# Gated DeltaNet block on one core: transpositions of k, q and v in one run for both heads of a pair, and longer steps between the interleaved pieces

## The chip, the cores and the metric

One Trainium2 chip; the kernel runs on one of its cores. The metric is the device time of one execution, in microseconds (us). The engines are called PE (matrix multiplication), DVE (vector), ACT (scalar), POOL (GpSimd) and SP (which issues most transfers).

## The reference

One layer, sequence 512, width 2048, float32. Two branches read one normalised input; the change touches the first.

```python
h = rmsnorm(x, g_pre)
proj = h @ w_in                       # q, k, v, z_a, beta, decay, conv input, gates
q, k, v = split(silu(causal_depthwise_conv(qkv, w_conv_qkv)))   # 4 taps, 16 heads x 128
q, k = l2norm(q), l2norm(k)           # x * rsqrt(sum(x*x) + EPS)
beta, g = sigmoid(b_raw), -exp(a_log) * softplus(a_raw + dt_bias)
# chunks of 64, per head: decay mask exp(gc_i - gc_j), triangular inverse T,
# then over 8 chunks: v_new = u - w S;  o = q_dec S + (q k^T * decay) v_new;
#                     S = S * exp(g_last) + k_end^T v_new
y_a = (rmsnorm(o_a) * silu(z_a)) @ w_br_a
u = causal_depthwise_conv(glu(...), w_dw) + b_dw                # 31 taps
y_b = (silu(layernorm(u)) * silu(z_b)) @ w_br_b
mixed = (gate_a * y_a + gate_b * y_b) @ w_out
x = x + rmsnorm(mixed)
x = x + rmsnorm(sigmoid(x @ w_ple_gate) * (p @ w_ple_proj))
```

## The kernel before, in words

**The large products.** Every float32 product is made of three passes in a reduced type: a weight tile is split into a rounded high part (L127, ACT) and the rest, the low part (L128, DVE; from the end of the heads on for a while POOL). `gemm_cm` makes one 128 x 512 output tile of the input projection, called g, from 16 blocks of weights with three matmuls each: L184 (high by high), L186 (high by low of the input hl), L188 (low of the weights by high). That is 48 matmuls to a tile. Two PSUM buffers (pool gps) take turns as g.

**What runs between them.** After each of these matmuls `tick()` is called. Side jobs are Python generators, entered by `spawn(gen, period)`. Each tick counts down each generator; when its count is out, the generator writes its next piece of instructions and yields again. A plain `yield` waits for the generator's period (4 ticks for a pair of heads, 5 for the decays), `yield n` for n ticks. So the code between two yields stands in one place of the program, and a longer wait puts the next piece behind more matmuls of g. `finish("heads")` drains what is left of the heads at the end of their stage, with no matmul between the pieces. The layer under the kernel may then reorder the instructions of an engine within limits; `pin` keeps some in place.

**The heads.** Sixteen heads are worked through in eight pairs, one pair per eight g tiles (384 ticks). For the pair g, `group(g)` makes, in this order: transposed k of both heads (pk, 4 transpositions of 128 x 128 each), from which ACT takes squares (junk, summed into sk) and DVE makes ke; the powers nk on POOL; transposed q (pq) and its squares into sq; transposed v (pv) and from it vh; the products pg of k and q; a product of sq with a constant that swaps halves of partitions (pe), from which comes epsq; the triangular inverse (prod, VT); the products py, pz, pd; and then two `head_scan` generators side by side, the recurrence over eight chunks (psA, psB, psS). A scan ends with squares of O, their power (ors, POOL), four products with the gate z (O, L739), a transposition back (po, L744) and its copy with a factor (oa, L749). While a scan of one pair runs out, `group` of the next pair has begun: their pieces meet.

**Buffers in PSUM.** Two buffers of the pool wps are shared in turn by all of pk, pq, pv, pg, pe, pz, py, pd, po and by the tiles of the decays (ba_t, gc_ps, sw_ps, r_ps). A new user waits until the last reader of the second-last one is done. The four buffers of sps serve the recurrence.

**The decays.** `beta_decay` runs once, ahead of the first pair. It makes the decays, a swapped copy of them (sw_ps, L614) and then, for the eight pairs, a mask each: products tg on DVE and POOL, a matmul pair into r_ps (L633), a chain on DVE and ACT on E_mk, and a store to DRAM (e_dram). E_mk has one buffer.

**Behind the heads.** The 31-tap filter of the second branch is done channel block by channel block: on DVE in steps of one tap (uc, L954), for two blocks on POOL (uc, L973, with the products pr from ACT). Finished blocks are added up on POOL; the first of them is a copy (acc, L918).

Of the kernel before, what the change touches and what calls it, by code (L numbers as in the profile page):

```python
# [9 lines left out]
F32 = mybir.dt.float32  # L10
F32R = mybir.dt.float32r
AF = mybir.ActivationFunctionType
ALU = mybir.AluOpType
AX = mybir.AxisListType.X

P = 128
T = 512
NTT = T // P
# [4 lines left out]
EPS = 1e-6  # L23
# [26 lines left out]
C_SWAP = 128  # L50
# [31 lines left out]
def _body(ctx, tc, A, out):  # L82
    nc = tc.nc
    PSUM = bass.MemoryType.PSUM
    mm = nc.tensor.matmul
# [12 lines left out]
    ident = cst[:, C_ID:C_ID + P]  # L98
# [7 lines left out]
    def cc(col, n=P):  # L106
        return cst[:, col:col + n]
# [406 lines left out]
    hd = heads_ctx.enter_context(tc.tile_pool(name="hd", bufs=2))  # L514
    wps = heads_ctx.enter_context(tc.tile_pool(name="wps", bufs=2, space=PSUM))
    sps = heads_ctx.enter_context(tc.tile_pool(name="sps", bufs=4, space=PSUM))
# [22 lines left out]
    def beta_decay(ps):  # L539
# [39 lines left out]
        s = tl("s")  # L579
# [29 lines left out]
        eg = tl("eg")  # L609
        nc.scalar.activation(eg, gcf, AF.Exp)  # L610
        nc.vector.tensor_scalar(neg_eg.rearrange("p t h -> p (t h)"), eg, -1.0, None, ALU.mult)
        yield
        pw = wps.tile([P, T], F32, tag="w", name="sw_ps")
        mm(pw[:, 0:n], cc(C_SWAP), eg, start=True, stop=True)  # L614
        nc.vector.tensor_copy(eg_sw.rearrange("p t h -> p (t h)"), pw[:, 0:n])
# [7 lines left out]
        for gi in range(NH // 2):  # L623
            tg = []
            for eng, src, tag in ((nc.vector, gh, "ke"), (nc.gpsimd, gl, "vh")):
                t = hd.tile([P, 2, NTT, 64], F32R, tag=tag, name="tg", bufs=2)
                gv = src.bitcast(F32)[:, :, 2 * gi:2 * gi + 2].rearrange("p t h -> p h t")
                eng.tensor_tensor(t, tri, gv.unsqueeze(3).broadcast_to([P, 2, NTT, 64]), ALU.mult)
                tg.append(t.rearrange("p h t i -> p (h t i)"))
            yield  # L630
            yield
            pr = wps.tile([P, T], F32, tag="w", name="r_ps")
            mm(pr, blk, tg[0], start=True, stop=False)  # L633
            mm(pr, blk, tg[1], start=False, stop=True)
            yield
            ed = hd.tile([P, 2, NTT, 64], F32, tag="W", name="E_mk", bufs=1)
            gcv = gc[:, :, 2 * gi:2 * gi + 2].rearrange("p t h -> p h t")
            nc.vector.tensor_tensor(ed, pr.rearrange("p (h t i) -> p h t i", h=2, i=64),
                                    gcv.unsqueeze(3).broadcast_to([P, 2, NTT, 64]), ALU.subtract)
            edf = ed.rearrange("p h t i -> p (h t i)")  # L640
            nc.vector.tensor_scalar(edf, edf, 0.0, None, ALU.min)
            nc.scalar.activation(edf, edf, AF.Exp)
            nc.vector.tensor_tensor(ed.rearrange("p h t i -> p (h t) i"), ed.rearrange("p h t i -> p (h t) i"),
                                    cst[:, C_TRI:C_TRI + 64].unsqueeze(1).broadcast_to([P, 8, 64]), ALU.mult)
            yield
            nc.sync.dma_start(e_dram[gi], edf)
# [38 lines left out]
    def head_scan(g, hh, G):  # L685
        h = 2 * g + hh
        st = hstate[h]
        kq, ke, vh = st["kq"], G["ke"][hh], G["vh"][hh]
        c_all = G["c"]
# [4 lines left out]
        for c in range(8):  # L694
            tt, par = divmod(c, 2)
            a, b = 64 * par, 64 - 64 * par
            x = hh * NTT + tt
# [30 lines left out]
        junk = hd.tile([P, P], F32, tag="junk", name="junk", bufs=1)  # L728
# [8 lines left out]
        yield  # L737
        for tt in range(NTT):
            nc.vector.scalar_tensor_tensor(O[:, tt, :], O[:, tt, :], rs2[:, tt:tt + 1], z[:, tt, :], ALU.mult, ALU.mult)  # L739
        yield  # L740
        yield
        po = wps.tile([P, NTT, 2, 64], F32, tag="w", name="po")
        for tt in range(NTT):
            nc.tensor.transpose(po[:, tt].rearrange("p x i -> p (x i)"), O[:, tt, :], ident)  # L744
# [7 lines left out]
    def group(g):  # L752
        G = dict(ke=[], vh=[])
# [3 lines left out]
        sq = hd.tile([P, 8], F32, tag="sq", name="sq")  # L757
        nk = hd.tile([P, 8], F32, tag="nk", name="nk")
        c_all = hd.tile([P, 8], F32, tag="c_all", name="c_all")
        W = hd.tile([P, 8, 2, 64], F32, tag="W", name="W", bufs=1)  # L760
        Ec = E.rearrange("p h t i -> p (h t) i")
        junk = hd.tile([P, P], F32, tag="junk", name="junk", bufs=1)
        heads = []
        for hh in range(2):
            h = 2 * g + hh
            heads.append((hh, h, slice(hh * NTT, (hh + 1) * NTT), hstate[h]["kq"], hstate[h]["kc"], hstate[h]["vc"]))
        for hh, h, s4, kq, kc, vc in heads:
            pk = wps.tile([P, NTT, P], F32, tag="w", name="pk")
            for tt in range(NTT):
                nc.tensor.transpose(pk[:, tt, :], kc[:, tt * P:(tt + 1) * P], ident)  # L770
            yield
            for tt in range(NTT):
                nc.scalar.activation(junk, pk[:, tt, :], AF.Square, accum_out=sk[:, hh * NTT + tt:hh * NTT + tt + 1])
            ke = hd.tile([P, NTT, P], F32, tag="ke", name="ke", bufs=2)
            nc.vector.tensor_tensor(ke, pk, ek[:, :, h:h + 1].broadcast_to([P, NTT, P]), ALU.mult)
            G["ke"].append(ke)
            nc.vector.tensor_scalar(sk[:, s4], sk[:, s4], EPS, None, ALU.add)
            nc.gpsimd.tensor_tensor(nk[:, s4], sk[:, s4], half_c[:, 0:NTT], ALU.pow)
            rk = hd.tile([P, NTT], F32, tag="rk", name="rk")
            nc.vector.reciprocal(rk, sk[:, s4])  # L780
            nc.vector.tensor_tensor(c_all[:, s4], rk, beta[:, :, h], ALU.mult)
            nc.gpsimd.tensor_tensor(Ec[:, s4, :], E[:, hh], c_all[:, s4].unsqueeze(2).broadcast_to([P, NTT, 64]), ALU.mult)
        for hh, h, s4, kq, kc, vc in heads:
            yield
            pq = wps.tile([P, NTT, P], F32, tag="w", name="pq")
            for tt in range(NTT):
                nc.tensor.transpose(pq[:, tt, :], kq[:, tt, 1:3, :].rearrange("p x i -> p (x i)"), ident)
            yield
            for tt in range(NTT):
                nc.scalar.activation(junk, pq[:, tt, :], AF.Square, accum_out=sq[:, hh * NTT + tt:hh * NTT + tt + 1])  # L790
        for hh, h, s4, kq, kc, vc in heads:
            pv = wps.tile([P, NTT, P], F32, tag="w", name="pv")
            for tt in range(NTT):
                nc.tensor.transpose(pv[:, tt, :], vc[:, tt * P:(tt + 1) * P], ident)
            yield
            vh = hd.tile([P, NTT, P], F32, tag="vh", name="vh", bufs=2)
            nc.vector.tensor_tensor(vh, pv, nk[:, s4].unsqueeze(2).broadcast_to([P, NTT, P]), ALU.mult)
            G["vh"].append(vh)
        yield
        pgs = []  # L800
        for hh, h, s4, kq, kc, vc in heads:
            pg = wps.tile([P, NTT, 2, 64], F32, tag="w", name="pg")
            for c in range(8):
                tt, par = divmod(c, 2)
# [5 lines left out]
        for hh, h, s4, kq, kc, vc in heads:  # L810
            nc.vector.scalar_tensor_tensor(W[:, s4, 0, :], pgs[hh][:, :, 0, :], -1.0, Ec[:, s4, :], ALU.mult, ALU.mult)
            nc.vector.tensor_tensor(W[:, s4, 1, :], pgs[hh][:, :, 1, :], Ec[:, s4, :], ALU.mult)
        pe = wps.tile([P, T], F32, tag="w", name="pe")
        mm(pe[:, 0:8], cc(C_SWAP), sq, start=True, stop=True)
        epsq = hd.tile([P, 8], F32, tag="epsq", name="epsq")
        nc.vector.tensor_scalar(epsq, pe[:, 0:8], EPS, EPS * P, ALU.add, ALU.mult)
        G.update(epsq=epsq, c=c_all)
        U = W[:, :, 0, :]
        QK = W[:, :, 1, :]

# [665 lines left out]
    ps = run(("P1",), stepper(gen))  # L1486
# [212 lines left out]
```

## Time and profile before

| | |
|---|---|
| median of 3 runs | 2446.0 us (2445.83 to 2446.65) |
| the profiled execution | 2447.55 us |
| its span in the trace | 2445.8 us, granted PE clock 0.998 |
| PE busy | 2414.0 us, 99% |
| PE's weight loads | 1985.5 us, 81% |
| DVE, ACT, POOL busy | 1792.4 (73%), 1208.8 (49%), 507.0 (21%) |

How to read the rows. In the timeline a row has the start in us from the span's beginning, the busy time, the engine, the line, the operation and "output<-inputs", and the shapes; "x4" means four in a row as one entry. A bracket gives the idle time of the engine just ahead of the row and what ended it. In the page's list of groups the numbers behind "|" are busy time in us and mean ns of one, and behind the next "|" the idle time ahead of the group and what ended most of it. In the list of waits stand the waiting instruction, what released it, and then total us, count and the longest. In a row of windows stand the stretch and its length, for each engine the busy time with the number of instructions in brackets (PE, weight loads, DVE, ACT, POOL), the granted PE clock, the DMA share and GB/s. A line such as "L775 ... x16: 681/688/693, 636.6 to 1391.9" gives the count, the shortest, middle and longest in ns, and the first and last start.

### The profile page before, as it was taken

To read this page: it belongs to the slowest core of one execution; us is meant where nothing else is said; L and a number is where in the kernel's file an instruction comes from. 1 tells how busy PE (TensorE), PEld (TensorE's weight loads), DVE (VectorE), ACT (ScalarE), POOL (GpSimd) and SP (SyncE) were. 2 spreads that over 40 slices of the span, in tenths; PEclk is the share of its full clock that TensorE was granted. 3 is DMA by queue.
4 is the path that set the end of the run, shared out by engine and by line. 5 is a ranking of instruction groups with operands and counts; after the bars stand their busy time and mean duration, and the time that the engine had idled before them with its cause. 6 is when DMAs were issued, how large, how long until landed. Compare 5 with 4: busy or idle time off the path is not lost.

```text
span 2445.8 us, 33732 instructions
## 1 busy us (share of the span) xinstructions
PE 2414.0 (99%) x11962; PEld 1985.5 (81%) x11962; DVE 1792.4 (73%) x3345; ACT 1208.8 (49%) x2357; POOL 507.0 (21%) x531
## 2 busy tenths in 40 slices
PE   8999999999999999999999998999999999999998
PEld 7888888887888888888888887888887888787886
DVE  7877888777677676867777678998998654667644
ACT  6455544554655656455555544454324533554532
POOL 0001110013213021132300005998740000000000
PEclk9999999999999999999999999999999999999999
DMA  7577776666536263556622222443534333665552
GB/s 270 162 199 199 202 201 208 207 162 204 175 119 185 87 185 93 171 168 178 181 90 90 67 91 79 138 137 104 170 118 166 131 122 99 232 216 173 188 173 77
DMA packets 145289, 380.21 MB, mean 155 GB/s; under 512 B 16352, under 2 KB 24800, under 8 KB 145120
## 3 DMA queue, kind: packets, MB, share of 16 engines
q1 hardware_dynamic: 119008, 319.32, 39.4%
q0 software_dynamic: 23808, 54.54, 10.3%
q10 hardware_dynamic: 2304, 4.20, 0.5%
q8 instruction: 94, 1.54, 0.3%
q14 instruction: 75, 0.61, 0.1%
HBM read 329.75 MB, written 48.23 MB: 155 GB/s over the span
## 4 chain that ended last, share of the span: by engine, by line
PE 89%; DVE 3%; POOL 2%; DMA 2%; issue 2%; ACT 2%; SPq 0%; POOLq 0%; DVEq 0%; ACTq 0%
PE g L186 13%; PE g L188 13%; PE g L184 13%; PE zp L423 6%; PE zp L421 6%; PE zp L422 5%; PE yp L1090 4%; PE yp L1094 4%; PE yp L1092 4%; PE f L1382 2%; PE f L1383 2%; PE f L1384 2%; PE f L1548 2%; PE f L1549 2%; PE f L1550 2%
## 5 line engine op out<-in xcount | busy, mean ns | idle before, releaser
L188 PE MATMUL g<-hh,w 128*128 128x512 f32 x1536 | 610.6, 397 | 4.1 <-POOL w L128 4.1
L186 PE MATMUL g<-hl,w 128*128 128x512 f32 x1536 | 611.3, 398 | 0.0
L184 PE MATMUL g<-hh,w 128*128 128x512 f32 x1536 | 609.5, 397 | 0.0
L127 ACT CAST w<-raw 128x512 fp32r<-128x512 f32 x588 | 357.9, 618 | 446.8 <-PE g L188 172.8
L128 DVE TENSOR_TENSOR w<-raw,w 128x512 fp32r<-128x512 f32 x464 | 321.5, 700 | 169.2 <-ACT w L127 166.6
L188 PEld LDWEIGHTS g<-hh,w 128*128 128x128 f32 x1536 | 289.8, 189 | 61.5 <-POOL w L128 5.4
L186 PEld LDWEIGHTS g<-hl,w 128*128 128x128 f32 x1536 | 289.6, 189 | 55.8 <-issue 1.4
L184 PEld LDWEIGHTS g<-hh,w 128*128 128x128 f32 x1536 | 289.9, 189 | 54.7 <-ACT w L127 0.9
L954 DVE SCALAR_TENSOR_TENSOR uc<-up,vec,uc 128x506 f32<-128x506 f32 (+29 forms) x390 | 284.0, 734 | 11.9
L128 POOL TENSOR_TENSOR w<-raw,w 128x512 fp32r<-128x512 f32 x124 | 161.4, 1314 | 136.7 <-DVE uc L954 74.5
L656 DVE SCALAR_TENSOR_TENSOR cv<-g,vec,cv 128x511 f32<-128x511 f32 x144 | 106.4, 739 | 27.2 <-ACT cv L654 26.6
L1090 PE MATMUL yp<-w,uh 128*128 128x512 f32 x256 | 100.2, 392 | 0.7 <-DVE gt L1102 0.7
L1094 PE MATMUL yp<-w,ul 128*128 128x512 f32 x256 | 100.1, 392 | 0.0
L1090 PE MATMUL yp<-w,oh 128*128 128x512 f32 x256 | 100.0, 393 | 0.0
L1092 PE MATMUL yp<-w,uh 128*128 128x512 f32 x256 | 100.0, 391 | 0.0
L1092 PE MATMUL yp<-w,oh 128*128 128x512 f32 x256 | 99.6, 389 | 0.0
L1094 PE MATMUL yp<-w,ol 128*128 128x512 f32 x256 | 99.1, 389 | 0.0
L842 DVE TENSOR_TENSOR prod<-UT,VT 128x2 f32<-128x2 f32 (+30 forms) x248 | 88.4, 356 | 6.5
L1006 POOL DMA_DIRECT2D wsum<-in_w_out x96 | 76.1, 847 | 71.2 <-DMA wsum<-in_w_out 32.9
L1326 POOL TENSOR_TENSOR rmsm<-totm,mhalf_c 128x2 f32<-128x2 f32 x2 | 2.4, 1198 | 378.3 <-DVE totm L1324 378.3
L973 POOL TENSOR_TENSOR uc<-uc,pr 128x511 f32<-128x511 f32 (+29 forms) x60 | 77.8, 1297 | 3.7 <-ACT pr L972 2.5
L1382 PE MATMUL f<-wsp,oph 128*128 128x512 f32 x192 | 75.6, 394 | 1.7 <-ACT wsp L1363 1.7
(386 smaller groups left out, 4952.5 us busy)
## 6 DMA issues: line engine op xcount, KB each, us to landing
raw<-in_w_in SPq DMA_DIRECT2D x194, 512.0 KB, 3.4
wsum<-in_w_out POOLq DMA_DIRECT2D x96, 256.0 KB, 5.4
raw<-in_w_ple_gate SPq DMA_DIRECT2D x40, 512.0 KB, 3.5
wo_sums<-wsum POOLq DMA_DIRECT2D x64, 256.0 KB, 4.1
raw<-in_w_br_a SPq DMA_DIRECT2D x32, 512.0 KB, 3.4
raw<-in_w_br_b SPq DMA_DIRECT2D x32, 512.0 KB, 3.3
raw<-in_w_ga SPq DMA_DIRECT2D x24, 512.0 KB, 4.7
raw<-in_w_gb SPq DMA_DIRECT2D x24, 512.0 KB, 4.5
```

The source lines that it names most:

```text
L127: nc.scalar.copy(hi, rq)
L128: low_part[0].tensor_tensor(lo, rq, hi.bitcast(F32), ALU.subtract)
L184: mm(ps, wh, rh, start=(k == 0), stop=False)
L186: mm(ps, wh, rl, start=False, stop=False)
L188: mm(ps, wl, rh, start=False, stop=(k == NK - 1))
L421: mm(ps[pr][t], lh, wh, start=q + n == 0, stop=False)
L423: mm(ps[pr][t], lh, wl, start=False, stop=q == 3 and n == 1)
L954: pin(nc.vector.scalar_tensor_tensor(y[:, s:], u[:, 0:T - s], vv(w0 + TAPS - 1 - s), y[:, s:], ALU.mult, ALU.add))
L1090: mm(ps[tt], lh[:, b], wh, start=k == 0, stop=False)
L1092: mm(ps[tt], lh[:, b], wl, start=False, stop=False)
L1094: mm(ps[tt], ll[:, b], wh, start=False, stop=k == NK - 1)
L1382: mm(ps, lh, wh[:, c], start=kk == 0, stop=False)
```

## The change

In `group`, a helper `turn(name, part)` writes the transpositions of k, q or v for both heads of the pair without a yield between them. The yields between the pieces become 6, 10, 6, 12 and 6 ticks in place of plain ones. The swap product pe and epsq move from behind pg into the piece of v, and pe's buffer comes from sps in place of wps. In `beta_decay` the swap of the decays comes 14 ticks after the piece before it, not 5, and each mask's r_ps 16 ticks after its products, not 10. In `head_scan`, po comes 16 ticks after the products O, not 8.

```diff
--- before.py
+++ after.py
@@ -609,7 +609,7 @@
         eg = tl("eg")
         nc.scalar.activation(eg, gcf, AF.Exp)
         nc.vector.tensor_scalar(neg_eg.rearrange("p t h -> p (t h)"), eg, -1.0, None, ALU.mult)
-        yield
+        yield 14
         pw = wps.tile([P, T], F32, tag="w", name="sw_ps")
         mm(pw[:, 0:n], cc(C_SWAP), eg, start=True, stop=True)
         nc.vector.tensor_copy(eg_sw.rearrange("p t h -> p (t h)"), pw[:, 0:n])
@@ -627,8 +627,7 @@
                 gv = src.bitcast(F32)[:, :, 2 * gi:2 * gi + 2].rearrange("p t h -> p h t")
                 eng.tensor_tensor(t, tri, gv.unsqueeze(3).broadcast_to([P, 2, NTT, 64]), ALU.mult)
                 tg.append(t.rearrange("p h t i -> p (h t i)"))
-            yield
-            yield
+            yield 16
             pr = wps.tile([P, T], F32, tag="w", name="r_ps")
             mm(pr, blk, tg[0], start=True, stop=False)
             mm(pr, blk, tg[1], start=False, stop=True)
@@ -737,8 +736,7 @@
         yield
         for tt in range(NTT):
             nc.vector.scalar_tensor_tensor(O[:, tt, :], O[:, tt, :], rs2[:, tt:tt + 1], z[:, tt, :], ALU.mult, ALU.mult)
-        yield
-        yield
+        yield 16
         po = wps.tile([P, NTT, 2, 64], F32, tag="w", name="po")
         for tt in range(NTT):
             nc.tensor.transpose(po[:, tt].rearrange("p x i -> p (x i)"), O[:, tt, :], ident)
@@ -764,11 +762,19 @@
         for hh in range(2):
             h = 2 * g + hh
             heads.append((hh, h, slice(hh * NTT, (hh + 1) * NTT), hstate[h]["kq"], hstate[h]["kc"], hstate[h]["vc"]))
+        def turn(name, part):
+            two = []
+            for hh, h, s4, kq, kc, vc in heads:
+                ps = wps.tile([P, NTT, P], F32, tag="w", name=name)
+                for tt in range(NTT):
+                    nc.tensor.transpose(ps[:, tt, :], part(tt, kq, kc, vc), ident)
+                two.append(ps)
+            return two
+
+        pks = turn("pk", lambda tt, kq, kc, vc: kc[:, tt * P:(tt + 1) * P])
+        yield 6
         for hh, h, s4, kq, kc, vc in heads:
-            pk = wps.tile([P, NTT, P], F32, tag="w", name="pk")
-            for tt in range(NTT):
-                nc.tensor.transpose(pk[:, tt, :], kc[:, tt * P:(tt + 1) * P], ident)
-            yield
+            pk = pks[hh]
             for tt in range(NTT):
                 nc.scalar.activation(junk, pk[:, tt, :], AF.Square, accum_out=sk[:, hh * NTT + tt:hh * NTT + tt + 1])
             ke = hd.tile([P, NTT, P], F32, tag="ke", name="ke", bufs=2)
@@ -780,19 +786,22 @@
             nc.vector.reciprocal(rk, sk[:, s4])
             nc.vector.tensor_tensor(c_all[:, s4], rk, beta[:, :, h], ALU.mult)
             nc.gpsimd.tensor_tensor(Ec[:, s4, :], E[:, hh], c_all[:, s4].unsqueeze(2).broadcast_to([P, NTT, 64]), ALU.mult)
+        yield 10
+        pqs = turn("pq", lambda tt, kq, kc, vc: kq[:, tt, 1:3, :].rearrange("p x i -> p (x i)"))
+        yield 6
         for hh, h, s4, kq, kc, vc in heads:
-            yield
-            pq = wps.tile([P, NTT, P], F32, tag="w", name="pq")
             for tt in range(NTT):
-                nc.tensor.transpose(pq[:, tt, :], kq[:, tt, 1:3, :].rearrange("p x i -> p (x i)"), ident)
-            yield
-            for tt in range(NTT):
-                nc.scalar.activation(junk, pq[:, tt, :], AF.Square, accum_out=sq[:, hh * NTT + tt:hh * NTT + tt + 1])
+                nc.scalar.activation(junk, pqs[hh][:, tt, :], AF.Square, accum_out=sq[:, hh * NTT + tt:hh * NTT + tt + 1])
+        yield 12
+        pvs = turn("pv", lambda tt, kq, kc, vc: vc[:, tt * P:(tt + 1) * P])
+        pe = sps.tile([P, P], F32, tag="s", name="pe")
+        mm(pe[:, 0:8], cc(C_SWAP), sq, start=True, stop=True)
+        yield 6
+        epsq = hd.tile([P, 8], F32, tag="epsq", name="epsq")
+        nc.vector.tensor_scalar(epsq, pe[:, 0:8], EPS, EPS * P, ALU.add, ALU.mult)
+        G.update(epsq=epsq, c=c_all)
         for hh, h, s4, kq, kc, vc in heads:
-            pv = wps.tile([P, NTT, P], F32, tag="w", name="pv")
-            for tt in range(NTT):
-                nc.tensor.transpose(pv[:, tt, :], vc[:, tt * P:(tt + 1) * P], ident)
-            yield
+            pv = pvs[hh]
             vh = hd.tile([P, NTT, P], F32, tag="vh", name="vh", bufs=2)
             nc.vector.tensor_tensor(vh, pv, nk[:, s4].unsqueeze(2).broadcast_to([P, NTT, P]), ALU.mult)
             G["vh"].append(vh)
@@ -810,11 +819,6 @@
         for hh, h, s4, kq, kc, vc in heads:
             nc.vector.scalar_tensor_tensor(W[:, s4, 0, :], pgs[hh][:, :, 0, :], -1.0, Ec[:, s4, :], ALU.mult, ALU.mult)
             nc.vector.tensor_tensor(W[:, s4, 1, :], pgs[hh][:, :, 1, :], Ec[:, s4, :], ALU.mult)
-        pe = wps.tile([P, T], F32, tag="w", name="pe")
-        mm(pe[:, 0:8], cc(C_SWAP), sq, start=True, stop=True)
-        epsq = hd.tile([P, 8], F32, tag="epsq", name="epsq")
-        nc.vector.tensor_scalar(epsq, pe[:, 0:8], EPS, EPS * P, ALU.add, ALU.mult)
-        G.update(epsq=epsq, c=c_all)
         U = W[:, :, 0, :]
         QK = W[:, :, 1, :]
```

In the built programs an ordinary pair has 39 runs of small matmuls before and 36 after, and r_ps follows r_ps every 26 ticks, not 20. Three places in the order of the engines, with the buffer numbers in the names:

PE, the meeting of the first and the second pair (po is the end of the first, all others belong to the second; matmuls of g stand in the places left out). Before:

```order
L744 MATMUL po_6730<-cst_75,O_6325 128x128 x4
L744 MATMUL po_6735<-cst_75,O_6331 128x128 x4
...
L770 MATMUL pk_6779<-cst_75,kc_6065 128x128 x4
...
L770 MATMUL pk_6800<-cst_75,kc_6445 128x128 x4
...
L787 MATMUL pq_6826<-cst_75,kq_6067 128x128 x4
...
L787 MATMUL pq_6843<-cst_75,kq_6447 128x128 x4
...
L794 MATMUL pv_6865<-cst_75,vc_6278 128x128 x4
...
L794 MATMUL pv_6876<-cst_75,vc_6755 128x128 x4
...
L807 MATMUL pg_6891<-kq_6067 64x128 x8
L807 MATMUL pg_6900<-kq_6447 64x128 x8
...
L814 MATMUL pe_6920<-sq_6774,cst_75 128x8
```

After (L770 is the line of all transpositions in the helper):

```order
L770 MATMUL pk_6763<-cst_75,kc_6063 128x128 x4
L770 MATMUL pk_6768<-cst_75,kc_6425 128x128 x4
...
L742 MATMUL po_6805<-cst_75,O_6334 128x128 x4
...
L742 MATMUL po_6810<-cst_75,O_6340 128x128 x4
...
L770 MATMUL pq_6830<-cst_75,kq_6065 128x128 x4
...
L770 MATMUL pq_6835<-cst_75,kq_6427 128x128 x4
...
L770 MATMUL pv_6875<-cst_75,vc_6273 128x128 x4
L770 MATMUL pv_6880<-cst_75,vc_6739 128x128 x4
L798 MATMUL pe_6885<-sq_6758,cst_75 128x8
...
L816 MATMUL pg_6904<-kq_6065 64x128 x8
L816 MATMUL pg_6913<-kq_6427 64x128 x8
```

Both pk now stand ahead of both po, and each pq behind the po of the same number; pe stands with pv.

DVE at the same place (cv are the steps of a 4-tap filter on a finished g, w a low part, O and oa the end of the first pair). Before:

```order
L739 SCALAR_TENSOR_TENSOR O_6325<-O_6325,ors2_6699,za_6326 128x128 x4
...
L739 SCALAR_TENSOR_TENSOR O_6331<-O_6331,ors2_6703,za_6332 128x128 x4
...
L749 TENSOR_SCALAR oa_6744<-po_6730,vec_76 128x4x64 x2
L749 TENSOR_SCALAR oa_6747<-po_6735,vec_76 128x4x64 x2
L656 SCALAR_TENSOR_TENSOR cv_6750<-g_6602,vec_76,cv_6750 128x511
L128 TENSOR_TENSOR w_6763<-raw_6758,w_6763 128x512
L656 SCALAR_TENSOR_TENSOR cv_6750<-g_6602,vec_76,cv_6750 128x510
L775 TENSOR_TENSOR ke_6792<-pk_6779,ek_4983 128x512
L656 SCALAR_TENSOR_TENSOR cv_6750<-g_6602,vec_76,cv_6750 128x509
...
L775 TENSOR_TENSOR ke_6813<-pk_6800,ek_4983 128x512
...
L797 TENSOR_TENSOR vh_6874<-pv_6865,nk_6775 128x512
L797 TENSOR_TENSOR vh_6885<-pv_6876,nk_6775 128x512
```

After:

```order
L655 SCALAR_TENSOR_TENSOR cv_6734<-g_6588,vec_76,cv_6734 128x511
L128 TENSOR_TENSOR w_6747<-raw_6742,w_6747 128x512
L655 SCALAR_TENSOR_TENSOR cv_6734<-g_6588,vec_76,cv_6734 128x510
L781 TENSOR_TENSOR ke_6783<-pk_6763,ek_4983 128x512
L655 SCALAR_TENSOR_TENSOR cv_6734<-g_6588,vec_76,cv_6734 128x509
...
L747 TENSOR_SCALAR oa_6820<-po_6805,vec_76 128x4x64
...
L781 TENSOR_TENSOR ke_6795<-pk_6768,ek_4983 128x512
...
L747 TENSOR_SCALAR oa_6820<-po_6805,vec_76 128x4x64
...
L747 TENSOR_SCALAR oa_6823<-po_6810,vec_76 128x4x64 x2
...
L806 TENSOR_TENSOR vh_6896<-pv_6875,nk_6759 128x512
L801 TENSOR_SCALAR epsq_6894<-pe_6885 128x8
L806 TENSOR_TENSOR vh_6898<-pv_6880,nk_6759 128x512
```

The copies oa have moved from ahead of the filter and both ke to places between and behind the ke; epsq comes between the two vh.

POOL behind the heads, around the first copy into acc (uc and pr are the filter's block on POOL, w a low part). Before:

```order
L973 TENSOR_TENSOR uc_14138<-uc_14138,pr_14211 128x509
L973 TENSOR_TENSOR uc_14138<-uc_14138,pr_14241 128x508
L128 TENSOR_TENSOR w_14249<-raw_14247,w_14249 128x512
L128 TENSOR_TENSOR w_14252<-raw_14247,w_14252 128x512
L973 TENSOR_TENSOR uc_14138<-uc_14138,pr_14277 128x507
L128 TENSOR_TENSOR w_14294<-raw_14292,w_14294 128x512
L918 COPY acc_14450<-uc_13756 128x512
L128 TENSOR_TENSOR w_14297<-raw_14292,w_14297 128x512
L973 TENSOR_TENSOR uc_14138<-uc_14138,pr_14313 128x506
L128 TENSOR_TENSOR w_14336<-raw_14334,w_14336 128x512
```

After:

```order
L128 TENSOR_TENSOR w_14248<-raw_14246,w_14248 128x512
L128 TENSOR_TENSOR w_14251<-raw_14246,w_14251 128x512
L977 TENSOR_TENSOR uc_14137<-uc_14137,pr_14276 128x507
L128 TENSOR_TENSOR w_14293<-raw_14291,w_14293 128x512
L128 TENSOR_TENSOR w_14296<-raw_14291,w_14296 128x512
L977 TENSOR_TENSOR uc_14137<-uc_14137,pr_14312 128x506
L922 COPY acc_14456<-uc_13764 128x512
L128 TENSOR_TENSOR w_14335<-raw_14333,w_14335 128x512
L128 TENSOR_TENSOR w_14338<-raw_14333,w_14338 128x512
L977 TENSOR_TENSOR uc_14137<-uc_14137,pr_14346 128x505
```

One low part and one step of the filter that followed the copy now stand ahead of it.

## The prediction

> **What bounds the kernel now.** I read the page first, then who waited for whom on PE, then the timeline at the places that the change touches.
>
> ```profile
> span 2445.8 us, 33732 instructions
> PE 2414.0 (99%) x11962; PEld 1985.5 (81%) x11962; DVE 1792.4 (73%) x3345; ACT 1208.8 (49%) x2357; POOL 507.0 (21%) x531
> ...
> L188 PE MATMUL g<-hh,w 128*128 128x512 f32 x1536 | 610.6, 397 | 4.1 <-POOL w L128 4.1
> ```
>
> PE is the bound from end to end. Work on the other engines costs nothing until PE waits for it, so every term below is a wait or a restart of PE. These are PE's waits at the places in question:
>
> ```profile
> PE g L188 <- POOL w L128: 4.1, 2, 3.5
> PE po L744 <- DVE O L739: 3.1, 4, 1.0
> ...
> PE r_ps L633 <- DVE E_mk L638: 0.7, 1, 0.7
> ...
> PE sw_ps L614 <- ACT ba_s L610: 0.6, 1, 0.6
> PE pv L794 <- ACT junk L790: 0.2, 1, 0.2
> ```
>
> The changed places own little: some 4.6 us in total. The four po waits are all in the last pair of heads. The largest wait, 3.5 us at L188, lies behind the heads, but its queue is one that the change reorders.
>
> **The runs of transpositions.** PE, an ordinary pair (the second):
>
> ```profile
> 738.82 1.04 PE L744 MATMUL po<-cst,O 128*128 128x128 f32 x8
> 739.61 0.48 PE L188 MATMUL g<-hh,w 128*128 128x512 f32 x1
> 739.92 0.40 PE L184 MATMUL g<-hh,w 128*128 128x512 f32 x1
> ...
> 741.52 0.60 PE L770 MATMUL pk<-cst,kc 128*128 128x128 f32 x4
> 741.88 0.48 PE L186 MATMUL g<-hl,w 128*128 128x512 f32 x1
> 742.20 0.40 PE L188 MATMUL g<-hh,w 128*128 128x512 f32 x1
> 742.43 0.40 PE L184 MATMUL g<-hh,w 128*128 128x512 f32 x1
> ```
>
> The first column is the start. A run of eight takes 0.79 us to the next g matmul and 0.31 to the one after; plain ones follow each other in 0.23. A run of four takes 0.36 and 0.32. Eight transpositions with two matmuls behind them are 0.79 + 0.31 + 0.23 = 1.33 us as one run, 2 x (0.36 + 0.32) = 1.36 as two. So a run saved is worth 0.03 us at most. The built programs have 39 runs of small matmuls per pair before and 36 now: 3 x 8 x 0.03 = 0.7 as the upper end, nothing as the lower. I take -0.4, as the four hundredths are near the rounding. The swap product pe costs the same two passes wherever it stands; its new home sps takes it out of the wps rotation.
>
> The Trainium skill ("TensorE: Matmul & The Clock Gate", section Single matmul latency) gives a lone matmul a fixed 166 ns beyond its columns, which a stream hides. If each run paid that, 24 fewer runs would be worth, as an estimate from that page, 4.0 us, and the sum would be 3.6 us lower. The rows above disagree: a run costs hundredths.
>
> **The masks.** The chain of one mask ends in a store, and the next mask waits for its buffer:
>
> ```profile
> 582.62 0.68 DVE L638 TENSOR_TENSOR E_mk<-r_ps,gc 128x512 f32<-128x512 f32 x1
> ...
> 632.14 0.69 DVE L638 TENSOR_TENSOR E_mk<-r_ps,gc 128x512 f32<-128x512 f32 x1 [0.98 <-DMA e_dram<-E_mk]
> ...
> 610.37 0.39 PE L184 MATMUL g<-hh,w 128*128 128x512 f32 x1
> 611.51 0.47 PE L633 MATMUL r_ps<-tg,blk 128*128 128x512 f32 x1 [0.75 <-DVE E_mk L638]
> ```
>
> Seven steps take 49.5 us, 7.07 each. PE offered a step every 20 matmuls, 20 x 0.23 + 0.5 = 5.1 us, ran out of wps buffers once and lost 1.14 - 0.23 = 0.9 us. At 26 matmuls it offers one every 6.5 us. With two buffers' head start (14 us) the lag of 7 x 0.57 = 4 us never reaches PE. Gain 0.9; bounds 0.9 and 0. The chain now ends about 1.4 us later, since its first step starts 13 matmuls (3.0 us) later and no longer sits behind DVE; the second pk is ordered behind it. The longer wait at the swap of decays moves nothing: sw_ps stands behind the same ACT instructions and after the same g matmul in both orders, so its 0.6 us stays. The first pair's pv wait (0.2 us) gives way to waits of the same kind; I take 0 with 0.6 either way.
>
> **The meeting of two pairs.** In seven of eight pairs the po of the finished pair now stands behind the k of the next, and all these share the two wps buffers: po[0] needs pk[0] read out, po[1] pk[1], pq[0] po[0], pq[1] po[1]. Before, eight matmuls stood between po and pk and nobody waited. What a pk needs to come free:
>
> ```profile
> 742.22 0.28 ACT L773 ACTIVATE junk<-pk 128x128 f32<-128x128 f32 x1 [0.22 <-PE pk L770]
> ...
> 745.57 0.20 ACT L773 ACTIVATION_READ_ACCUMULATOR junk<-pk 128x1 f32 x1
> ...
> 743.83 0.69 DVE L775 TENSOR_TENSOR ke<-pk,ek 128x512 f32<-128x512 f32 x1 [0.28 <-ACT junk L773]
> 744.43 0.74 DVE L656 SCALAR_TENSOR_TENSOR cv<-g,vec,cv 128x509 f32<-128x509 f32 x1
> ...
> 740.50 0.87 DVE L749 TENSOR_SCALAR oa<-po,vec 128x256 f32<-128x256 f32 x2
> ...
> 641.38 0.66 PE L794 MATMUL pv<-cst,vc 128*128 128x128 f32 x4 [0.23 <-ACT junk L790]
> ...
> 745.18 0.60 PE L787 MATMUL pq<-cst,kq 128*128 128x128 f32 x4
> ...
> L775 DVE TENSOR_TENSOR ke<-pk,ek x16: 681/688/693, 636.6 to 1391.9; 128x512 f32<-128x512 f32 x16
> ```
>
> Times from pk's start at 741.52: squares from 0.70, ke only after four of them, 2.31 to 3.00. ACT and DVE hold the same instructions ahead of these now, so pk[0] is free at 3.00. PE comes to po[0] after eight g matmuls: 0.79 + 0.31 + 7 x 0.23 = 2.71. It waits 0.29, and a run after a wait takes 0.06 longer (0.66 against 0.60): 0.35 us. Then po[1], seven matmuls on, at 3.05 + 0.36 + 0.32 + 6 x 0.23 = 5.11. The eighth square ends at 4.25, the second ke would at 5.04: even. pq[0] follows at 5.79; oa of the first head, whose second half stands behind that ke, ends by 5.75: even. pq[1] at 7.39, oa of the second at about 7.42. Three even ones, 0.1 together. 0.45 x 7 = +3.1 us. The lower end is 0 (the buffer is handed over before ke ends). The upper takes one more DVE instruction of 0.60 in front of one of the even ones: 0.95 x 7 = 6.7. Behind that, pv comes 13 matmuls (3.4 us) after pq[1] and needs only the four squares of that head; eight with a cast between them took 742.22 to 745.77. pg comes ten after pv, 2.6 us: covered.
>
> **The last pair.** Its end is issued in one go when the stage closes; five g matmuls more now cover it, and half a step of the recurrence more lies in it.
>
> ```profile
> 738.05 1.14 DVE L739 SCALAR_TENSOR_TENSOR O<-O,ors,za 128x128 f32<-128x128 f32 x4 [1.12 <-POOL ors L735]
> ...
> 1486.03 2.16 DVE L739 SCALAR_TENSOR_TENSOR O<-O,ors,za 128x128 f32<-128x128 f32 x4 [1.19 <-POOL ors L735]
> ...
> 1486.48 1.29 POOL L128 TENSOR_TENSOR w<-raw,w 128x512 fp32r<-128x512 f32 x1 [0.49 <-ACT w L127]
> ```
>
> Four O products take 1.14 us in an ordinary pair and 2.16 beside POOL's L128. POOL now has both powers of the last pair next to each other, so the first four lose this companion: -1.0. The tighter recurrence may wait 0.3 more. I take -0.7; bounds -1.5 and +1.5.
>
> **The low part behind the heads.** POOL makes the low parts of weights (L128) there and also adds up filtered channels. Its copy acc waits for a whole channel on DVE, with the next low part behind it:
>
> ```profile
> 1495.02 3.50 POOL L973 TENSOR_TENSOR uc<-uc,pr 128x511 f32<-128x511 f32 x2 [2.47 <-ACT pr L972]
> ...
> 1510.25 1.72 POOL L128 TENSOR_TENSOR w<-raw,w 128x512 fp32r<-128x512 f32 x1
> 1519.40 0.61 POOL L918 COPY acc<-uc 128x512 f32<-128x512 f32 x1 [7.43 <-DVE uc L954]
> 1519.97 1.27 POOL L128 TENSOR_TENSOR w<-raw,w 128x512 fp32r<-128x512 f32 x1
> ...
> 1494.17 6.58 DVE L954 SCALAR_TENSOR_TENSOR uc<-sg,vec,uc 128x502 f32<-128x502 f32 x5
> ...
> 1507.51 11.83 DVE L954 SCALAR_TENSOR_TENSOR uc<-sg,vec,uc 128x493 f32<-128x493 f32 x12
> ...
> 1517.45 0.39 PE L186 MATMUL g<-hl,w 128*128 128x512 f32 x1
> 1521.29 0.79 PE L188 MATMUL g<-hh,w 128*128 128x512 f32 x1 [3.45 <-POOL w L128]
> ...
> 1526.96 0.40 PE L184 MATMUL g<-hh,w 128*128 128x512 f32 x1
> ...
> 1521.30:1526.00 4.70, 4.70 (x11) 3.73 (x12) 4.49 (x7) 0.04 (x1) 4.70 (x4) 0.50 0.65 217
> ```
>
> From 1495.02 POOL does ten pieces of 1.70 us, then stands until 1519.40. A DVE channel step takes 0.75 us alone and 1.69 beside POOL: two alone and three beside make the 6.58 of the first row, nine and three the 11.83 of the second. Now POOL has a low part and a step more ahead of the copy (12 x 1.70 = 20.4 us), all starts 5 x 0.23 = 1.15 later, and DVE has 22 steps and an evacuation left, not 21. Before, DVE did 1.1 steps alone and 10.1 beside POOL until POOL stood at 1512.0; the other 9.8 end at 1519.4 by this reckoning, and 1519.34 is what happened. Now it does 1.1 and 12.1 until 1516.6; the other 8.8 take 6.6, the evacuation 0.6, which is 1523.8. Copy and low part take 1.9 as before (1519.34 to 1521.24): 1525.7. PE needs this low part 12 matmuls later than the old one: 1517.68 + 2.73 = 1520.4. Wait 5.3 against 3.6: +1.7. The granted clock is 0.50 in the row after the wait (PEclk, third from the end): the 13 intervals from 1521.29 to 1526.96 take 5.67 us, 2.7 above 13 x 0.23. I keep that. Bounds: wait and slow clock gone, -6.3; two more DVE steps beside POOL, +3.
>
> **Sum.** -0.4 - 0.9 + 0 + 3.1 - 0.7 + 1.7 = +2.8 us. The profiled execution took 2447.55 (its span and 1.75 around it), so 2450.35 there; that execution stands 1.55 above the median of 2446.0, so I predict 2448.8. A measurement of this kernel can tell about 0.2%, 4.9 us, from no change.
>
> **Rivals.** (a) The meeting costs nothing because the hand-over is earlier than I read it: without 3.1 the time is 2445.7. The pq of before, which started at 745.18 without a wait, 0.66 after ke was done, can't exclude it. (b) Slower: at the meeting the order on DVE lets one 0.60 us instruction in front of the second ke, and po[1], pq[0] and pq[1] wait in turn: 6.7 in place of 3.1, 2452.4. From 0.74 us per meeting on it is slower by more than 0.2%. Against it: ke took 681 to 693 ns in all sixteen heads (the last row above), so DVE was met in the same state each time. (c) Faster: the channel on DVE is done before PE asks for the low part, as POOL's extra pieces run while DVE waits for something else; wait and slow clock vanish: 2448.8 - 1.7 - 6.3 = 2440.8. It needs the channel 5.3 us earlier than worked out. (d) The long wait breaks in two: the evacuation that stands between the last channel steps holds a g bank, so PE stops twice, and the clock may stay up: 2448.8 - 2.7 = 2446.1.
>
> For (d) the Trainium skill ("TensorE: Matmul & The Clock Gate", section Why this matters for your kernels) says that idle gaps beyond about 3 us bring half rate. By that rule the trace agrees so far: 3.45 us of idle time was followed by 0.50.
>
> **Chances.** Forecast 0.46, with its own range 2446.5 to 2451.5; (a) 0.18; (b) 0.16; (c) 0.08; (d) 0.12. Slower by over 0.2%: (b) and 0.06 of the forecast's upper tail, 0.22. Faster: (c), 0.08. Within: 0.70. The range reaches from between (c) and (a), 2443.5, to just past (b), 2453.
>
> **What would show it.** PE waits at the first po of seven pairs for ke, 0.3 us each; no r_ps wait; sw_ps still 0.6; acc on POOL near 1523.8 plus what PE has lost until then; a clock row near 0.5 behind it. Wrong if po finds its buffer free, or if the low part's wait is much off 5.3.

## The result and the profile after

The changed kernel takes 2467.5 us (median of 4 runs, 2466.6 to 2470.2) against 2446.0: ratio 1.009, 95% interval 1.0078 to 1.0102. It is 21.5 us slower; the forecast was +2.8 and a range up to 2453.

The waits of PE in the profile after (what waited, on what, total us, times, longest):

```profile
PE py L867 <- DVE Tc L861: 3.9, 9, 1.0
PE g L188 <- POOL w L128: 3.2, 1, 3.2
PE po L742 <- DVE O L738: 3.2, 2, 1.7
PE pz L870 <- DVE Tc L861: 2.0, 7, 0.3
PE po L742 <- DVE ke L781: 2.0, 7, 0.3
PE psB L708 <- DVE Xz L704: 1.9, 6, 0.3
...
PE sw_ps L614 <- ACT ba_s L610: 0.7, 1, 0.7
```

What was forecast is there: seven waits of po for ke, 0.3 us each, sw_ps much as before (0.6 us before, 0.7 now), no r_ps. What was not is py, pz and psB: the inverse and the recurrence, which the change doesn't touch.

Listed waits are only part of such a loss, since a run that is broken by a wait also costs its restart: in the rows below, py and pz lose 1.45 us with 0.68 us of listed waits. So I added up, for the stretch of 3820 g matmuls from the decays on, all time between the starts of PE instructions beyond 0.227 us per g matmul, and booked it to the small matmuls at which it lies ("g": between two g matmuls only). This table is worked out from all PE rows of each profile, in us:

```
kernel      masks  k,q,v,po,pg  py,pz,pd  recurrence     g     sum
before       7.5      52.3        25.2       86.8      10.9   182.7
after        6.7      55.1        36.2       91.6      13.7   203.1
```

Of +20.4, the inverse's products have +11.0, the recurrence +4.8, the meetings of pairs +2.7, g itself +2.8, the masks -0.8. (The spans of the two profiles differ by 19.0; the remaining 1.4 us came back outside this stretch.) Per ordinary pair: py, pz, pd 3.11 to 4.6, recurrence 10.82 to 11.6, k to pg and po 5.92 to 6.4.

The inverse in the second pair, first PE, then DVE, and before also ACT. Before:

```profile
797.91 0.39 PE L186 MATMUL g<-hl,w 128*128 128x512 f32 x1
798.23 0.69 PE L863 MATMUL py<-Tc,W 32*32 32x32 f32 x32
798.85 1.15 PE L866 MATMUL pz<-W,Tc 64*64 64x64 f32 x32
799.93 0.50 PE L188 MATMUL g<-hh,w 128*128 128x512 f32 x1
...
793.48 0.67 DVE L850 STREAM_TRANSPOSE Vd<-VT 128x256 f32<-128x256 f32 x1
794.08 0.71 DVE L656 SCALAR_TENSOR_TENSOR cv<-g,vec,cv 128x511 f32<-128x511 f32 x1
...
797.04 1.37 DVE L857 STREAM_TRANSPOSE Tc<-VP 32x256 f32<-32x256 f32 x3
...
794.19 2.83 ACT L856 COPY VP<-Vd 32x256 f32<-32x256 f32 x4 [3.26 <-DVE Vd L850]
```

After:

```profile
800.43 0.39 PE L184 MATMUL g<-hh,w 128*128 128x512 f32 x1
800.88 0.21 PE L867 MATMUL py<-Tc,W 32*32 32x32 f32 x2
801.49 0.69 PE L867 MATMUL py<-Tc,W 32*32 32x32 f32 x30 [0.39 <-DVE Tc L861]
802.25 0.30 PE L870 MATMUL pz<-W,Tc 64*64 64x64 f32 x2
802.83 1.14 PE L870 MATMUL pz<-W,Tc 64*64 64x64 f32 x30 [0.29 <-DVE Tc L861]
803.90 0.51 PE L186 MATMUL g<-hl,w 128*128 128x512 f32 x1
...
794.82 0.74 DVE L655 SCALAR_TENSOR_TENSOR cv<-g,vec,cv 128x511 f32<-128x511 f32 x1
...
797.30 0.75 DVE L655 SCALAR_TENSOR_TENSOR cv<-g,vec,cv 128x509 f32<-128x509 f32 x1
797.96 0.42 DVE L847 TENSOR_REDUCE VT<-prod 128x8 f32<-128x256 f32 x1
...
798.88 0.67 DVE L854 STREAM_TRANSPOSE Vd<-VT 128x256 f32<-128x256 f32 x1
800.30 0.43 DVE L861 STREAM_TRANSPOSE Tc<-VP 32x256 f32<-32x256 f32 x1 [0.75 <-ACT VP L860]
801.00 0.44 DVE L861 STREAM_TRANSPOSE Tc<-VP 32x256 f32<-32x256 f32 x1 [0.26 <-ACT VP L860]
```

From the g matmul ahead of py to the one behind pz it was 2.02 us and is 3.47. Before, the three filter steps cv of the finished g tile stood behind Vd: they filled the time in which DVE has to wait for ACT's copies VP. Now the pair's inner pieces stand 8 matmuls later against the end of the tile, the cv stand ahead of the inverse's last step, and DVE idles behind Vd. py finds one of four Tc.

### The profile page after: what moved, and what is told of

Its sections match the earlier page's. It is cut to its first block, busy times and chain, and to the rows that moved or that the text cites. A ratio compares the mean times of both kernels' runs of the same rounds, so it can differ in the third digit from the quotient of the medians.

```text
span 2464.8 us, 33736 instructions
## 1 busy us (share of the span) xinstructions
PE 2423.4 (98%) x11962; PEld 1991.0 (81%) x11962; DVE 1784.4 (72%) x3345; ACT 1215.7 (49%) x2359; POOL 510.6 (21%) x531
## 4 chain that ended last, share of the span: by engine, by line
PE 81%; DVE 12%; issue 3%; ACT 2%; POOL 1%; DMA 1%; SPq 0%; DVEq 0%; POOLq 0%; ACTq 0%
PE g L188 10%; PE g L186 10%; PE g L184 10%; PE zp L423 6%; PE zp L421 6%; PE zp L422 6%; PE yp L1098 5%; PE yp L1096 5%; PE yp L1094 5%; DVE prod L846 3%; DVE w L128 3%; PE f L1386 2%; PE f L1387 2%; PE f L1388 2%; DVE VT L847 2%
## 5 line engine op out<-in xcount | busy, mean ns | idle before, releaser
L958 DVE SCALAR_TENSOR_TENSOR uc<-up,vec,uc 128x511 f32<-128x511 f32 (+29 forms) x390 | 285.2, 734 | 12.4
L1010 POOL DMA_DIRECT2D wsum<-in_w_out x96 | 75.7, 827 | 67.5 <-DMA wsum<-in_w_out 36.2
```

The costliest lines, as they stand in the source:

```text
L958: pin(nc.vector.scalar_tensor_tensor(y[:, s:], u[:, 0:T - s], vv(w0 + TAPS - 1 - s), y[:, s:], ALU.mult, ALU.add))
```

## The experiments

Each kernel ran with the kernel before on the same chip; medians in us, ratios with 95% intervals. Four theories are named in the expectations: P (phase: the pieces behind pg stand 8 matmuls later against the ends of the g tiles), M (the meeting of pairs), R (the runs of eight or pe's new pool), L (later is worse, wherever the tile ends).

**The shift alone** (kernel before):

```diff
-        yield
+        yield 12
         pgs = []
```

> The kernel before, with 12 ticks in place of 4 ahead of pg: pg and all behind it stand 8 matmuls of g later, at the same places against the ends of the g tiles as in the changed kernel. No run of eight, no po behind pk, no changed wait in the masks. Theory P (phase: behind pg every piece stands later against the evacuations of g tiles, which then go ahead of the inverse and into the recurrence on DVE): py and pz wait for Tc 0.5 to 0.8 us in each pair, half clock behind some of them (1.5 us each), scans 1.3 us longer: 7 or 8 pairs x 2.0 to 2.4 = +14 to +19, 2460 to 2465. Theory M (meeting: the loss comes from po behind both pk in the shared wps buffers and from the runs of eight): no change, 2445 to 2449.

Measured: 2469.7 against 2447.0, ratio 1.0087 (1.007 to 1.0104). A loss as large as the change's, without a run of eight and with po ahead of pk. But it is not made up alike. By the sums of the table above, py to pd rise from 25.2 to 33.3 us and the recurrence from 86.8 to 92.2, which is 13.6 together and just below what P had expected (14 to 19); k to po rise from 52.3 to 59.3, as now the next pair's pk waits for oa in seven pairs, and the masks by 1.5. So P's terms appear without the change's meeting of pairs, but this run has a costlier meeting of its own, and that its total is so near to the change's is in part luck. What speaks against M as the main cause is the table: in the changed kernel the meeting has +2.7 of +20.4.

**po early again** (changed kernel):

```diff
-        yield 16
+        yield
+        yield
         po = wps.tile(...)
```

> The changed kernel with the old two plain yields (8 ticks) ahead of po: po of the old pair stands ahead of the new pair's k again, all else as changed. P: py and pz waits and longer scans stay, only the seven waits of po for ke (0.3 us each) and their breaks go: 2461 to 2465. M: most of the loss goes with the meeting: 2446 to 2452.

Measured: 2472.6, ratio 1.0099 (1.0084 to 1.0114): no gain. That alone does not rule out M, since the meeting was not removed but exchanged: po no longer waits for ke, the next pair's pk waits for oa, and k to po rise from 55.1 to 59.5 us. What stays is the loss of the inverse (py to pd 37.4 us, against 36.2) and of the recurrence (92.0, against 91.6), wherever po stands:

```profile
PE pk L771 <- DVE oa L748: 2.1, 7, 0.3
```

**The old place with all else of the change:**

```diff
-        yield 10
+        yield 8
         pqs = turn("pq", ...)
-        yield 12
+        yield 8
         pvs = turn("pv", ...)
-        yield
+        yield 2
         pgs = []
-        yield 16
+        yield
+        yield
         po = wps.tile(...)
```

> The changed kernel with the old 8 ticks ahead of po, and with 8, 8 and 2 ticks in place of 10, 12 and 4 in the group, so that pg stands 36 matmuls behind pk as before and not 44; runs of eight, pe in sps and the longer waits in the decays stay. P: py and pz wait as little as before, scans as before, one r_ps wait less: 2443 to 2447. Theory R (the runs of eight themselves, or pe in sps, cost the time): 2455 to 2467.

Measured: 2452.0 against 2447.0, ratio 1.0016 (1.0007 to 1.0025). Some 16 us of the loss are gone. This kernel differs from the one above only in the waits that put pq, pv, pg and all behind them back, and the two stand 20.6 us apart; so the place is the main cause, and M and R fall as such. The recurrence is back at 10.8 us a pair, py to pd at 3.11 in all pairs but the first (6.1). The 5 us that stay were not expected. From the table's sums: k to po +1.8, of which the waits of pq for ke, py to pd in the first pair +2.7, g +2.6, the masks -1.0.

```profile
PE pq L771 <- DVE ke L782: 2.0, 8, 0.3
...
PE py L868 <- DVE Tc L862: 1.6, 2, 0.9
```

**The waits of the decays alone** (kernel before):

```diff
-        yield
+        yield 14
         pw = wps.tile(...)
-            yield
-            yield
+            yield 16
             pr = wps.tile(...)
```

> The kernel before with the two longer waits of the decays alone (14 ticks ahead of sw_ps, 16 ahead of r_ps). All theories: the r_ps wait of 0.75 us goes, sw_ps keeps 0.6 to 0.7, 2444 to 2446. If the masks came too late for the first pair, pg's successors there would wait: 2447 or more.

Measured: 2447.8 against 2447.0, ratio 1.0004 (0.9995 to 1.0014): not told from no change. The profile shows a gain and a loss, though its execution took 2451.2 us, the longest of the ten. The r_ps wait is gone (masks 7.5 to 6.5), but the masks end later, the first pair's Vd with them (687.67, against 686.25), and its py waits twice, so that py to pd cost 5.18 us in this pair and not 3.38:

```profile
690.72 0.22 PE L862 MATMUL py<-Tc,W 32*32 32x32 f32 x2 [0.53 <-DVE Tc L856]
691.72 0.69 PE L862 MATMUL py<-Tc,W 32*32 32x32 f32 x30 [0.79 <-DVE Tc L856]
```

Behind it the clock falls to 0.50 (windows of that run; the clock is third from the end):

```profile
694.00:696.00 2.00, 2.00 (x6) 1.54 (x6) 0.53 (x1) 1.26 (x3) 0.00 (x0) 0.50 0.51 164
```

**The inverse's end ahead of the filter steps** (changed kernel):

```diff
-        owed, pace = 0.0, 2.6
+        owed, pace = 0.0, 2.4
...
-        yield 22
+        yield 31
         pz = wps.tile(...)
```

> The changed kernel, with the inverse's steps written at a pace of 2.4 in place of 2.6 and 31 ticks in place of 22 ahead of py and pz. pg keeps its late place, py (2 matmuls earlier) and the recurrence nearly keep theirs; only the last steps of the inverse (prod, Vd, Tc) move on DVE ahead of the filter steps cv of the g tile. Theory P, in its part on the inverse: py and pz no longer wait, the half clock behind them goes; what PE spends on py, pz and pd beyond g falls from 36 us to 25 to 27, the scans stay at 90 to 93: 2453 to 2457. Rival L (whatever comes later in the pair is late, wherever the g tile ends): the same waits, 2464 to 2469.

Measured: 2468.0 against 2447.1, ratio 1.0083 (1.007 to 1.0097). A miss in the time, which alone would fit L; half a hit in the mechanism: with pg in its late place, py to pd fell from 36.2 to 29.4 us as Vd went ahead of the filter steps, so the order on DVE does make most of their wait. But the recurrence rose from 91.6 to 95.7 and g from 13.7 to 18.4. The recurrence's psB now waits for VP from DVE and its psS for ACT. That this is the same work, moved out of the inverse's way into the recurrence's, is likely but not shown:

```profile
PE psB L708 <- DVE VP L888: 1.5, 7, 0.2
...
PE pz L870 <- DVE Tc L861: 1.3, 7, 0.2
PE psS L714 <- ACT vz L711: 1.3, 7, 0.2
```

**A shift by a whole tile** (kernel before):

```diff
-        yield
+        yield 52
         pgs = []
```

> The kernel before with 52 ticks in place of 4 ahead of pg: pg and all behind it stand a whole g tile (48 matmuls) later, so at the same place against the ends of tiles, but now the next pair's k and q run into the end of the recurrence. P: PE's time for py, pz, pd is 25 to 27 us again and for the scans 86 to 89, though it is six times the shift of 8; the crossing at the next pair may cost 0 to 1 us per pair of its own: 2446 to 2455. L: worse than the shift of 8: 2470 or more.

Measured: 2486.5, ratio 1.0161 (1.0147 to 1.0175). The time missed widely and alone would again fit L. By the table's sums +21.0 of it lie between k and po, as the crossing at the next pair is dear: po waited 15.2 us.

```profile
PE po L744 <- DVE O L739: 15.2, 11, 1.7
...
PE py L863 <- DVE Tc L857: 4.3, 6, 0.8
```

But the recurrence took 10.94 us a pair, against 11.6 with a shift of 8 and 10.82 with none: for it P holds and L falls. For py to pd the run is inconclusive by itself (3.2 to 3.3 us in two late pairs, 4.6 to 4.8 in the first five): Vd stands ahead of the three cv again, yet the inverse ends late against py.

One number orders these prices in the runs so far, worked out from the PE and DVE rows: how long after the start of the g matmul just ahead of py the last of the four Tc is done. Where it is at most 0.9 us, py to pd cost 3.11 (the ordinary pairs before). At 1.5 us they cost 3.75 (the run above, with the inverse's end ahead of the filter steps), at 2.0 us 4.2 (the shift of 8), at 2.35 us 4.6 (the changed kernel, and the shift by a whole tile in four of its first five pairs), and at 3.3 us 5.5 (the changed kernel's first pair). Two pairs into which a stretch of half clock fell cost more, 5.75 and 6.1. So a late Tc is what costs, not a late pg, and for the inverse too L falls; what held the inverse back in the shift by a whole tile stays open.

**The recurrence alone 8 matmuls later** (kernel before):

```diff
+        yield 8
         scanning[0] = g
```

> The kernel before with 8 ticks more ahead of the recurrence only: inverse, py, pz and pd stay in their places, the scans and po stand 8 matmuls later, as in the changed kernel; po and the next pair's k come as in the run with pg shifted by 8 (turn pieces 7.0 us a pair against 5.9). Per pair, PE's time beyond g, theory P: py, pz, pd 3.1 us (as before), scan 11.5 to 11.6 (10.8 before), so +0.75 and +1.05 in seven pairs: 2457 to 2461. Rival (the scans were only longer because py came late): scan 10.8, 2453 to 2455.

Measured: 2460.7 against 2446.5, ratio 1.0055 (1.0041 to 1.0069). Per pair: py to pd 3.11, recurrence 11.5, k to po 7.0, all as P said. So the recurrence pays for its own place, not for a late py, and the prices add. One such place in the changed kernel, third pair: filter steps cv and a low part stand between the recurrence's pieces on DVE, and psB waits for Xz. From the g matmul ahead of this psB to the second one behind it PE takes 1.28 us, 0.82 beyond two plain steps; the other psB runs of two in this pair cost 0.23 to 0.32 by the same reckoning. So some 0.5 of the 0.75 us that the recurrence loses in this pair lie here.

```profile
934.49 0.74 DVE L655 SCALAR_TENSOR_TENSOR cv<-g,vec,cv 128x509 f32<-128x509 f32 x1
...
936.56 1.14 DVE L128 TENSOR_TENSOR w<-raw,w 128x512 fp32r<-128x512 f32 x1
937.73 0.36 DVE L704 SCALAR_TENSOR_TENSOR Xz<-psA,neg_eg,vh 64x128 f32<-64x128 f32 x1
...
937.42 0.40 PE L186 MATMUL g<-hl,w 128*128 128x512 f32 x1
938.14 0.49 PE L708 MATMUL psB<-Xz,VP 128*128 128x128 f32 x2 [0.32 <-DVE Xz L704]
938.38 0.47 PE L188 MATMUL g<-hh,w 128*128 128x512 f32 x1
938.70 0.39 PE L184 MATMUL g<-hh,w 128*128 128x512 f32 x1
```

**The low part behind the heads, two ways** (kernel before). First the copy into acc kept at its place in the program:

```diff
-            nc.gpsimd.tensor_copy(acc[0], y)
+            pin(nc.gpsimd.tensor_copy(acc[0], y))
```

> The kernel before, with the first copy into acc kept at its place in the program on POOL (about ten instructions later), so that no low part stands behind it while it waits for DVE. If the wait of 3.5 us at L188 and the half clock behind it (2.7 us) both came from that copy: 2440 to 2442 against 2446 to 2447. If POOL's longer company slows DVE's filter by as much, no change: 2445 to 2448.

Measured: 2452.7 against 2447.1, ratio 1.0021 (1.0012 to 1.003): slower, outside both expectations. The copy no longer holds POOL, so POOL's filter runs on beside DVE's, DVE's steps take 31.71 us for 19 (before, 25.17 for 21), and the evacuation sg behind them comes so late that PE stands for 8.7 us:

```profile
1494.41 31.71 DVE L954 SCALAR_TENSOR_TENSOR uc<-sg,vec,uc 128x500 f32<-128x500 f32 x19
...
1527.53 0.77 PE L184 MATMUL g<-hh,w 128*128 128x512 f32 x1 [8.71 <-DVE sg L981]
```

So the copy seems only the place where the wait showed, and DVE beside POOL its cause; the next run tests that. POOL's filter begun later:

```diff
     def side_convs():
+        yield 120
         for _ in range(SIDE):
```

> The kernel before with the filter on POOL begun 120 ticks (27 us) later. If the wait of 3.5 us at L188 and the half clock behind it come from DVE's last filter steps running beside POOL's filter: DVE is done some 4 to 7 us earlier, the copy into acc with it, and 3 to 6 us go: 2440 to 2444 against 2446 to 2447. Rival (the low parts alone slow DVE as much, or the later filter on POOL is missed at the end): 2445 to 2449.

Measured: 2439.5 against 2446.5, ratio 0.9971 (0.996 to 0.9982): faster than both kernels. DVE's 21 steps take 20.79 us, the copy starts at 1514.23 and not at 1519.40, and PE does not wait for a low part there:

```profile
1493.38 20.79 DVE L954 SCALAR_TENSOR_TENSOR uc<-sg,vec,uc 128x502 f32<-128x502 f32 x21
...
1514.23 0.61 POOL L918 COPY acc<-uc 128x512 f32<-128x512 f32 x1 [5.91 <-DVE uc L954]
```

So the cause was DVE beside POOL. Not all of the gain lies there: in the profile the last pair's po cost 3.67 us in place of 5.18, and a stretch of half clock near 1490 took some 1.2 us back. At the low part the clock stays up, by the window there:

```profile
1515.00:1520.00 5.00, 5.00 (x24) 4.14 (x23) 4.81 (x7) 1.90 (x5) 5.00 (x5) 1.00 0.82 275
```

**A better place for the recurrence?** Two runs on the kernel before, in which an ordinary pair has 36 runs of small matmuls and not 39, with 25 in place of 28 in the recurrence. The first:

```diff
-        owed, pace = 0.0, 2.6
+        owed, pace = 0.0, 2.4
...
-        yield 22
+        yield 29
         pz = wps.tile(...)
...
-            nc.gpsimd.tensor_copy(acc[0], y)
+            pin(nc.gpsimd.tensor_copy(acc[0], y))
```

> The kernel before with the copy into acc kept in place as in the run above, the inverse at a pace of 2.4, and 29 ticks ahead of py: Tc is early, py stands 4 matmuls earlier, and the recurrence falls against the tile ends so that a pair has 32 runs of small matmuls, not 36. P: 4 breaks of about 0.1 us less in 7 or 8 pairs, -2 to -4 beside the copy's effect: 2436 to 2443. L: no effect of the place, as the copy alone.

Measured: 2468.3 against 2447.1, ratio 1.0084 (1.007 to 1.0098). The recurrence fell to 10.57 us a pair as expected; pz lost far more, since one of the four Tc now stood between the filter steps, and the pinned copy cost 9.6 us at sg:

```profile
PE g L184 <- DVE sg L981: 9.6, 1, 9.6
PE pz L866 <- DVE Tc L857: 9.0, 7, 1.5
```

The second, beside the later filter on POOL:

```diff
-        yield 8
+        yield 6
         pd = wps.tile(...)
...
-        yield 6
+        yield 4
         for par in range(2):
             r = slice(64 * par, 64 * par + 32)
...
     def side_convs():
+        yield 120
```

> As the run above, and the recurrence 4 matmuls earlier by two shorter waits around pd (6 and 4 ticks in place of 8 and 6), so that its runs fall between the ends of the g tiles as in the run with 29 ticks ahead of py (scan 10.57 us a pair against 10.8), with the inverse and py left where they were (3.1 us). P: 1.9 us less than the run above: 2438 to 2442. If pd or the first psB then wait for ACT's copies of VP: 2441 to 2446.

Measured: 2443.1 against 2446.5, ratio 0.9985 (0.9976 to 0.9994). Recurrence 10.6, py to pd 3.11, but k to po 6.65 against 5.92: less gained than the later filter alone gave. Every place that was moved paid somewhere else.

## Why the prediction was wrong

Its account of the change ended too early. The step that failed is the sentence "pg comes ten after pv, 2.6 us: covered", with which the paragraph on the meeting of two pairs closed: it asked whether pg's inputs were ready, and did not follow that pg now stands 44 matmuls behind pk and not 36, and with it the inverse, py, pz, pd, the recurrence and po. The tiles of g keep their places, so all of these move against the evacuations on DVE and ACT. That term was left out; it measures +11.0 for py to pd and +4.8 for the recurrence in the profiles, of which 2.1 lie in the first pair's py to pd, where the longer waits of the decays alone bring 1.8. Two stretches of half clock behind pz add 3.1 us in g. It could have been seen: on DVE, Vd stands ahead of three cv before, and behind them after.

The terms that the forecast did have came out near it: masks -0.8, k to po with the last pair +2.7, low part about +1.0, together +2.9 against +2.8. That they agree so well is partly luck, as single terms were off by up to 0.7.

Point by point:

- Meetings: 0.45 us each forecast, 0.48 measured (5.92 to 6.40 a pair), with the seven waits for ke. Right.
- Runs: no row speaks against hundredths; against P's prices they don't count.
- Masks: the r_ps wait went as forecast. That the lag "never reaches PE" holds for r_ps alone: the later masks delay the first pair, whose py to pd cost 5.49 us in place of 3.38.
- Swap of decays: 0.6 us before, 0.7 after. Right.
- Last pair: forecast -0.7. What PE spent on its po went from 5.18 to 4.85 us: right in sign, half the size.
- The rivals were all about the meeting or the low part. None had the pieces behind pg, so the range could not hold the time.
- Low part: forecast a wait of 5.3 in place of 3.6 us, and acc near 1523.8 plus what PE had lost. The rows after, PE and POOL:

```profile
1539.77 0.47 PE L184 MATMUL g<-hh,w 128*128 128x512 f32 x1 [1.43 <-DVE sg L985]
1543.72 0.79 PE L188 MATMUL g<-hh,w 128*128 128x512 f32 x1 [3.24 <-POOL w L128]
...
1541.83 0.61 POOL L922 COPY acc<-uc 128x512 f32<-128x512 f32 x1 [7.14 <-DVE uc L958]
```

and the window behind the wait:

```profile
1543.00:1545.00 2.00, 1.28 (x3) 1.09 (x4) 1.89 (x4) 0.00 (x0) 2.00 (x3) 0.50 0.62 214
```

The wait came in two parts, 1.43 and 3.24, as rival (d) had it, yet the clock fell to 0.50 all the same. The place cost about 1 us more than before (forecast 1.7). What PE had lost until then: the same g matmul starts at 1500.22 before and at 1518.46 after, 18.2 us later. So the forecast puts the copy at 1542.0; it came at 1541.83.

What stays open: the 5 us that stay in the run with the old place are booked (first pair, pq, g). The waits of the decays alone bring 1.8 of the first pair's 2.7 and a stretch of half clock; pq was not tested apart. Of the recurrence's 0.7 us a pair some 0.5 lie at one psB, by one pair's rows; no run changed that step alone. No run kept po late with pg in its old place.

## What to carry to other kernels

When side work is paced by ticks of a main loop, a changed wait moves everything behind it against the loop's own periodic work. So follow the change to the end of the period, and look in the built order for what changes places on the engine that feeds the last step, not only at the edited lines. Work that fills another engine's latency can cost more than its own time when it moves: here, ahead of Vd, the filter steps delayed the chain and left the hole empty. And where a wait points to a queue, look for the engine behind it: pinning the copy made it worse, taking the competitor away removed it.

## What the runs showed of the hardware

The granted clock fell to half without a long wait. In the second pair after, PE waited 0.39 and 0.29 us by the rows above, and between 800.88 and 803.90 had only small matmuls; then:

```profile
800.00:804.00 4.00, 3.19 (x69) 2.36 (x67) 2.76 (x6) 3.87 (x8) 0.09 (x1) 1.00 0.00 0
804.50:807.50 3.00, 3.00 (x8) 2.33 (x8) 1.89 (x3) 2.11 (x4) 0.00 (x0) 0.50 0.52 175
...
912.00:916.00 4.00, 3.17 (x68) 2.34 (x67) 2.96 (x6) 3.87 (x8) 0.00 (x0) 1.00 0.00 0
916.00:920.00 4.00, 4.00 (x47) 3.07 (x45) 2.90 (x5) 2.79 (x6) 0.00 (x0) 1.00 0.59 170
```

Clock 0.50 cost about 1.5 us there, while the third pair, with the same waits, kept 1.00; behind the fourth it fell again, from 1026.2 to 1029.5. In the clock records of all these traces a stretch at 0.50 between 560 and 1660 us lasts 3.41 us or two or three times that. The Trainium skill ("TensorE: Matmul & The Clock Gate", section A second HAM failure mode: psum-queue depth-cycling) tells of a kernel in which frequent short idles of PE made the clock swing between half and full rate; these rows are in line with it, and show that the same pattern need not do it each time. Whether the short waits or the small matmuls between them brought the fall, no run here tells apart.
